# Projecting and convolving the second SSD group's B and C ahead of the first group's tiles, in both halves of a hybrid transformer block

## The chip, the cores and the metric

The kernel runs on one core of one Trainium2 chip. The metric is the device time of one execution in microseconds (us), as the median of several runs. Five engines work side by side, each on its own queue of instructions: TensorE (PE in the profile; PEld is its weight load), VectorE (DVE), ScalarE (ACT), GpSimd (POOL) and SyncE (SP), which issues most of the DMAs. One instruction of an engine waits for the results that it reads from others; whatever stands behind it in the same queue waits with it.

## The reference

One layer of a streaming encoder on 1024 tokens of width 1024, in fp32. After an RMSNorm one projection feeds three groups of heads; their outputs are concatenated, projected, normed and added, and a gated feed-forward follows:

```python
h = rmsnorm(x, pre_mix_norm)
proj = h @ w_in                       # split into the inputs of the three mixers
att = swa_sink_alibi(a_q, a_k, a_v, attn_sinks)      # sliding-window attention, 4 heads
ssd = ssd_mixer(s_z, s_xbc, s_dt, ...)               # Mamba-2 SSD, 2 groups of 4 heads
gdn = gdn_mixer(g_qkv, g_z, g_b, g_a, ...)           # gated DeltaNet, 4 heads
mix = jnp.concatenate([att, ssd, gdn], axis=-1) @ w_out
x = x + rmsnorm(mix, post_mix_norm)
h = rmsnorm(x, pre_ffn_norm)
f = (silu(h @ w_gate) * (h @ w_up)) @ w_down
x = x + rmsnorm(f, post_ffn_norm)
```

In the SSD mixer, x, B and C go through a causal convolution of four taps and a SiLU. Then, for each group, `y_diag = (C B^T * decay) x` inside a chunk, a state of 128 x 64 for each head is carried from chunk to chunk and read by C, a skip `x * D` is added, the sum is gated by `silu(z)` and normed over the 256 channels of the group. The gated DeltaNet needs the inverse of a lower triangular 128 x 128 matrix for each head and chunk of tokens.

## The kernel before, in words

The tokens are done in two halves of 512, four tiles of 128 tokens each. Within a half all three mixers are computed; the output projection of half 0 is worked in between the attention tiles of half 1; the feed-forward runs at the end for both halves.

Every fp32 product is made of three matmuls: operands are split into a high part (`wh`, `hhi`) and a low part (`wl`, `hlo`), and high x high, high x low and low x high are summed (`gemm_rows`, L207 to L209, and `gemm`, L213 to L215: three matmuls for each block of 128 rows, eight blocks a product, so 24 matmuls). A weight piece is loaded by SP (`wr_...`, L182), its high part is made by ACT (L183) and its low part in turn by POOL and DVE (L184), all under a high priority. So mm_B, mm_C and mm_x are 24 matmuls of 512 columns for one block of 128 channels of B, C or x, mm_z is 24 matmuls of 256 columns for each of four tiles of tokens, and mm_aq, mm_ak and mm_av are the attention's projections.

The order of emission in a half is a string of steps, `ORD` (L32 and L33), one for each half. Its letters: K the gated DeltaNet's keys and queries, V its values, G0 to G3 its scan over tiles; S0 and S1 the blocks of SSD group 0 and 1 (B, C, two blocks of x, then the gate z); s00 to s03 the tiles of group 0, s10 to s13 those of group 1; A the attention's projections, a0 to a3 its tiles, N the norm of the next half, O half 0's output projection. A scheduler then places each engine's instructions by a simulated timeline in which the place of emission is the priority: work that is emitted earlier goes first when it is ready, and later work fills gaps. So what stands in the string is a preference, and the order on each engine has to be looked up.

What the prediction speaks of, by lines:

- `conv_block` (L337 to L354): the product, a copy `cb` with three carried columns (ACT L344, POOL L343 or L346), the last tap with the bias (ACT L348), three taps on DVE (L350), a tanh on ACT (L353) and the gate on DVE (L354).
- `gate_rows` (L356 on): mm_z for each tile of tokens, a tanh on ACT (L363) and the gate on DVE (L364). The product's two PSUM buffers (`ps_mm`) are free again only after these.
- `decay_mats` (L439 on): the matmuls D_s (L444, L448) for two tiles of tokens and four heads, and exponentials on ACT (L453), which write E_s.
- `ssd_tile` (L659 to L725): transposes of x and B and the product C B^T into one PSUM buffer, tp_x (L688 to L690); ACT copies (L692, L694); DVE multiplies the four E_s blocks of a tile by dt and C B^T (L696, "the four E_s"); PE's y (L703, four small matmuls from E_s and xs, and L707 with the state); POOL's xw and xd (L698, L699); sz (L712), the new state (L714, or L716 and L717); y on DVE (L708, L718, L719), its square on ACT (L721), L722, a root on POOL (L167), L724 on DVE, and SP's store of the tile (L725). tp_x, D_s, y and sz take turns in two PSUM buffers (`ps_sd`).
- `gdn_diag` (L500 to L546): the inverse of the triangular matrices' diagonal blocks of 32, for all tiles of a half at once, almost all of it on DVE: a chain of products and sums in 15 steps for blocks of 16 (L525, L527), then a trip through DRAM (SP L529 to L532), then two products of four parts each (L538 with its sum L540), and back through DRAM (L545, and L558 in `gdn_inv`). `gdn_inv` (L548 on) transposes the result on DVE (L565) and makes the whole inverse of two tiles with small matmuls in a chain with ACT and DVE between them: lx (L577), lv, lX, lV.
- `gdn_scan` (L603 on): tp_v, PQ, Z, S (L642) with DVE steps between them; S is the state's product.
- `att_tile`: as (L746), the exps on ACT (L762), tp_p (L771), ao (L782).

The names in the profile carry h, t and g where the order prints them: y010 is the y of half 0, tile 1, group 0; B01 is B of half 0, group 1; Tst and Tpr are the inverse and its products.

Of the kernel before, what the change touches and what calls it, by code (L numbers as in the profile page):

```python
# [28 lines left out]
KQS = 2  # L29
SB = 2  # L30
WC = 544
ORD = ("K V G0 G1 G2 G3 S0 s00 s01 s02 s03 S1 s10 s11 s12 s13 A N a0 a1 a2 a3",  # L32
       "K V G0 G1 G2 G3 S0 s00 s01 s02 s03 S1 s10 s11 s12 s13 A a0 a1 O a2 a3")  # L33
STEPS = (1, 1, 2)
EARLY = (2, 4)
LEAD, SLEAD = 260, 90
# [33 lines left out]
def trunk(ctx, tc, a):  # L70
# [252 lines left out]
    def proj(h, hT, name, parts):  # L323
        wp = piece(f"{name}{h}", parts, KB)
        ps = ps_mm.tile([P, HT], F32, tag="mm", name=f"mm_{name}{h}")
        gemm(ps, wp, hT)
        return ps

    def proj_rows(h, hT, name, parts, width, evac):

        wp = piece(f"{name}{h}", parts, KB, width)
        for t in range(NT):
            ps = ps_mm.tile([P, HT], F32, tag="mm", name=f"mm_{name}{h}{t}")
            gemm_rows(ps[:, 0:width], hT, wp, slice(t * P, (t + 1) * P))
            evac(t, ps)

    def conv_block(h, hT, name, col, b, out):  # L337
        ps = proj(h, hT, name, [(0, w_in[:, col:col + P])])
        cb = cpool.tile([P, HT + 3], F32, tag="cb", name=f"cb_{name}{h}")
        if h == 0:  # L340
            pool.memset(cb[:, 0:3], 0.0)
        else:
            pool.tensor_copy(cb[:, 0:3], carry[:, b, :])  # L343
        act(out=cb[:, 3:], in_=ps, func=AF.Copy)  # L344
        if h == 0:
            pool.tensor_copy(carry[:, b, :], cb[:, HT:HT + 3])  # L346
        u = out
        act(out=u, in_=ps, func=AF.Identity, scale=wconv[:, b, 3:4], bias=wconv[:, b, 4:5])  # L348
        for i in (2, 1, 0):
            stt(out=u, in0=cb[:, i:i + HT], scalar=wconv[:, b, i:i + 1], in1=u,  # L350
                op0=ALU.mult, op1=ALU.add)
        th = cb[:, 0:HT]
        act(out=th, in_=u, func=AF.Tanh)  # L353
        stt(out=out, in0=th, scalar=1.0, in1=u, op0=ALU.add, op1=ALU.mult)  # L354

    def gate_rows(h, hT, name, parts, width, more=None):  # L356

        out = [ablk(f"{name}{h}{i}") for i in range(2)]
        tiles = [out[t // 2][:, t % 2 * 256:(t % 2 + 1) * 256] for t in range(NT)]

        def evac(t, ps):
            th = cpool.tile([P, HT + 3], F32, tag="cb", name=f"gth_{name}{h}{t}")[:, 0:256]
            act(out=th, in_=ps[:, 0:256], func=AF.Tanh, scale=0.5)  # L363
            stt(out=tiles[t], in0=th, scalar=1.0, in1=ps[:, 0:256], op0=ALU.add, op1=ALU.mult)  # L364
            if more is not None:
                more(t, ps)

        proj_rows(h, hT, name, parts, width, evac)
        return tiles

    def ablk(name):
        return apool.tile([P, HT], F32, tag="act", name=name)
# [418 lines left out]
    def half(h, hT, order):  # L791

        st = {}
# [23 lines left out]
            gdn_scan(st["grp"][t], st["v"])  # L817

        def ssd_blocks(g):
            blk = st[g] = {}  # L820
            for nm, b in (("B", 4 + g), ("C", 6 + g), ("x0", 2 * g), ("x1", 2 * g + 1)):
                blk[nm] = ablk(f"{nm}{h}{g}")
                conv_block(h, hT, f"{nm}{g}", O_X + b * P, b, blk[nm])
            blk["z"] = gate_rows(h, hT, f"z{g}",
                                 [(0, w_in[:, O_Z + g * 256:O_Z + (g + 1) * 256])], 256)

# [32 lines left out]
        def after():  # L859
            st["next"] = load_norm(h + 1)  # L860

        steps = dict(O=lambda: o0.append(block_first()), K=keys, V=values, G=scan, S=ssd_blocks, s=ssd, A=att_blocks, a=att, N=after)
        for step in order.split():
            steps[step[0]](*[int(c) for c in step[1:]])
        return st.get("next")

    pm_rows, o0 = [None, None], []
# [97 lines left out]
    for h in range(2):  # L965
        for t in range(GT):
            dma(vds[h][t].rearrange("h (b r) j -> (h b r) j", b=4).rearrange("(x r) j -> x r j", r=32)[:, 16:32, 0:16],
                S_bd[0:16].rearrange("p b l -> p (b l)")[:, 0:256].rearrange("p (r j) -> p r j", r=16))
    hT = half(0, hT, ORD[0])
    half(1, hT, ORD[1])  # L970
    mT_h0 = o0[0]
    for i in range(EARLY[0]):
# [91 lines left out]
    def silu(t):  # L1064
        act(out=t, in_=t, func=AF.Silu)
        return t
# [47 lines left out]
    for g in range(2):  # L1114
# [68 lines left out]
    for i in range(NP):  # L1183
        g = [silu(t) for t in ffn_pair("fg", wg, i, 0)]
# [182 lines left out]
```

## Time and profile before

| what | value |
|---|---|
| median of 3 runs | 1269.42 us (1267.31 to 1270.78) |
| the profiled execution | 1268.95 us |
| its span in the trace | 1267.2 us (1.75 us lie outside it) |
| mean granted TensorE clock | 0.982 |
| busy, TensorE / VectorE / ScalarE / GpSimd | 1218.1 / 913.7 / 574.8 / 217.8 us |

A row of a timeline has the start in us from the span's begin, the duration in us, the engine, the line, the instruction, output and inputs by the program's names, their shapes, and in brackets the idle time of the engine just before it and what ended that. "PE y L703 <- DVE E_s L696: 7.3, 2, 4.4" in the waits' view is: TensorE, at line 703, waited for VectorE's E_s of line 696, 7.3 us in all, twice, the longest 4.4. A row of windows has the stretch, its length, the busy time of PE, PEld, DVE, ACT and POOL with the number of instructions in brackets, the granted clock, the DMA engines' busy share and GB/s. In a group's row stand the shortest, median and longest duration in ns and the first and last start. Matmuls are pipelined: their spacing, not their duration, is what one costs. Group 0's tiles run from about 118 to 182 us in half 0 and from about 348 to 415 us in half 1.

### The profile page before, as it was taken

How to read it: one execution, taken by the hardware profiler on the slowest of the kernel's cores; microseconds unless marked ns; L12 is line 12 of the kernel's file. 1: busy time of each engine (PE TensorE's matmuls, PEld its weight loads, DVE VectorE, ACT ScalarE, POOL GpSimd, SP SyncE). 2: the span in 40 equal slices, each digit the busy share in tenths (PEclk: the TensorE clock that was granted, in tenths of full speed). 3: DMA queues.
4: the chain of work that ended last, by engine and by line, in shares of the span. 5: the costliest groups of instructions: out<-in, count | busy, mean ns of one | idle time of the engine just before them, and what ended most of it. 6: DMA issues, size and time to landing. Idle time of an engine off the chain costs nothing.

```text
span 1267.2 us, 18619 instructions
## 1 busy us (share of the span) xinstructions
PE 1218.1 (96%) x6384; PEld 1005.0 (79%) x6384; DVE 913.7 (72%) x1850; ACT 574.8 (45%) x1245; POOL 217.8 (17%) x313
## 2 busy tenths in 40 slices
PE   5999999999998999889999999999999999999997
PEld 4878778987787889878877888888888887888885
DVE  5677865796797385654668999886677666768885
ACT  7464435456443453553546443333433334444661
POOL 3244454233355432100000000000000000000000
PEclk9999989999998999979999999999999999999998
DMA  7333432143333222464573554542333367676315
GB/s 224 94 78 63 102 78 70 49 117 92 73 90 68 85 86 73 126 224 127 161 232 103 191 190 164 182 155 72 117 108 108 108 244 271 188 238 205 94 57 199
DMA packets 181795, 168.15 MB, mean 133 GB/s; under 512 B 52510, under 2 KB 137018, under 8 KB 181700
## 3 DMA queue, kind: packets, MB, share of 16 engines
q1 hardware_dynamic: 164276, 133.14, 36.0%
q10 hardware_dynamic: 17424, 33.82, 7.3%
q8 instruction: 50, 0.82, 0.3%
q14 instruction: 45, 0.37, 0.1%
HBM read 126.82 MB, written 40.11 MB: 132 GB/s over the span
## 4 chain that ended last, share of the span: by engine, by line
PE 82%; DVE 8%; DMA 6%; ACT 2%; issue 1%; SPq 1%; POOL 0%; ACTq 0%; DVEq 0%; POOLq 0%
PE mm_p L1238 5%; PE mm_p L1239 5%; PE mm_p L1240 5%; DMA wr_e<-in_ffn_w_gate_dram 1%; DMA x<-in_x_dram 1%; PE mm_o L208 1%; PE gram L490 1%; PE mm_o L209 1%; DMA yb<-in_ffn_w_down_dram 1%; PE mm_o L207 1%; PE y L703 1%; PE as L746 1%; PE ao L782 1%; PE mm_z L207 1%; DVE Tpr L538 1%
## 5 line engine op out<-in xcount | busy, mean ns | idle before, releaser
L167 POOL TENSOR_TENSOR rsq<-ssv,mhalf 128x1 f32<-128x1 f32 x32 | 20.0, 628 | 750.9 <-DVE ssv L260 740.3
L208 PE MATMUL mm_z<-wl_z,hhi_a 128*128 128x256 f32 x128 | 37.3, 291 | 1.6 <-DVE wl_z L184 1.6
L207 PE MATMUL mm_z<-wh_z,hhi_a 128*128 128x256 f32 x128 | 38.8, 303 | 0.0
L209 PE MATMUL mm_z<-wh_z,hlo_a 128*128 128x256 f32 x128 | 37.3, 291 | 0.0
L208 PE MATMUL mm_o<-wl_wo,hhi_m 128*128 128x256 f32 x128 | 36.7, 287 | 0.0
L209 PE MATMUL mm_o<-wh_wo,hlo_m 128*128 128x256 f32 x128 | 36.3, 284 | 0.0
L207 PE MATMUL mm_o<-wh_wo,hhi_m 128*128 128x256 f32 x128 | 36.3, 284 | 0.0
L183 ACT ACTIVATE wh_wo<-wr_wo 128x512 fp32r<-128x512 f32 x30 | 18.7, 631 | 27.2 <-PE mm_o L1133 8.2
L184 DVE TENSOR_TENSOR wl_wo<-wr_wo,wh_wo 128x512 fp32r<-128x512 f32 x22 | 15.2, 692 | 18.0 <-ACT wh_wo L183 17.9
L208 PEld LDWEIGHTS mm_z<-wl_z,hhi_a 128*128 128x128 f32 x128 | 25.6, 200 | 2.1 <-DVE wl_z L184 1.9
L207 PEld LDWEIGHTS mm_z<-wh_z,hhi_a 128*128 128x128 f32 x128 | 25.7, 201 | 0.7
L703 PE MATMUL y<-xs,E_s 128*128 128x64 f32 x128 | 19.1, 290 | 7.3 <-DVE E_s L696 7.3
L215 PE MATMUL mm_x<-hhi_a,wl_x 128*128 128x512 f32 x64 | 26.0, 406 | 0.0
L214 PE MATMUL mm_x<-hlo_a,wh_x 128*128 128x512 f32 x64 | 25.5, 398 | 0.0
L209 PEld LDWEIGHTS mm_z<-wh_z,hlo_a 128*128 128x128 f32 x128 | 25.4, 199 | 0.0
L213 PE MATMUL mm_x<-hhi_a,wh_x 128*128 128x512 f32 x64 | 25.3, 395 | 0.0
L703 PEld LDWEIGHTS y<-xs,E_s 128*128 128x128 f32 x128 | 18.1, 208 | 8.7 <-DVE E_s L696 7.7
L208 PEld LDWEIGHTS mm_o<-wl_wo,hhi_m 128*128 128x128 f32 x128 | 24.1, 189 | 1.0 <-issue 1.0
L209 PEld LDWEIGHTS mm_o<-wh_wo,hlo_m 128*128 128x128 f32 x128 | 24.1, 189 | 0.3 <-issue 0.3
L207 PEld LDWEIGHTS mm_o<-wh_wo,hhi_m 128*128 128x128 f32 x128 | 24.1, 188 | 0.3 <-ACT apT L772 0.3
L1131 PE MATMUL mm_o<-wh_wo,mhi 128*128 128x512 f32 x56 | 22.0, 393 | 0.3 <-ACT mhi L236 0.3
L207 PE MATMUL mm_gz<-wh_gz,hhi_a 128*128 128x272 f32 x64 | 20.8, 325 | 1.3 <-ACT dtn L378 1.3
(1801 smaller groups left out, 4380.8 us busy)
## 6 DMA issues: line engine op xcount, KB each, us to landing
wr_wo<-in_w_out_dram SPq DMA_DIRECT2D x32, 256.0 KB
x<-in_x_dram SPq DMA_DIRECT2D x8, 512.0 KB
wr_x<-in_w_in_dram SPq DMA_DIRECT2D x16, 256.0 KB
wr_z<-in_w_in_dram SPq DMA_DIRECT2D x16, 256.0 KB
res<-in_x_dram SPq DMA_DIRECT2D x8, 512.0 KB
resf<-x1d SPq DMA_DIRECT2D x8, 512.0 KB
mixn<-mixd SPq DMA_DIRECT2D x12, 256.0 KB
wr_e<-in_ffn_w_gate_dram SPq DMA_DIRECT2D x12, 256.0 KB
```

The lines of the kernel that those rows point to most:

```text
L167: pool.tensor_tensor(r[:, 0:n], v, mhalf[:, 0:n], op=ALU.pow)
L207: pe.matmul(ps, hi[:, tsl], whi, start=k == 0, stop=False)
L208: pe.matmul(ps, hi[:, tsl], wlo, start=False, stop=False)
L209: pe.matmul(ps, lo[:, tsl], whi, start=False, stop=k == len(wp) - 1)
L213: pe.matmul(ps, whi, hi, start=k == 0, stop=False)
L214: pe.matmul(ps, whi, lo, start=False, stop=False)
L215: pe.matmul(ps, wlo, hi, start=False, stop=k == len(wp) - 1)
L703: pe.matmul(yd[:, j], E[j], xs[:, j], start=True, stop=True)
L1131: pe.matmul(ps[t], hi[:, s], whi, start=k == korder[0], stop=False)
L1238: pe.matmul(ps[j], ah[:, s], bh, start=i == 0, stop=False)
L1239: pe.matmul(ps[j], ah[:, s], bl, start=False, stop=False)
L1240: pe.matmul(ps[j], al[:, s], bh, start=False, stop=i == NP - 1)
```

## The change

A new step, `B1`, stands behind S0 and ahead of group 0's tiles in the strings of both halves. It projects and convolves B and C of group 1 (a new function, `ssd_in`, that takes the kinds of blocks to do). When S1 comes, B and C are there, and only x and z of group 1 are done. Every block and every product stays as it is.

```diff
-ORD = ("K V G0 G1 G2 G3 S0 s00 s01 s02 s03 S1 s10 s11 s12 s13 A N a0 a1 a2 a3",
-       "K V G0 G1 G2 G3 S0 s00 s01 s02 s03 S1 s10 s11 s12 s13 A a0 a1 O a2 a3")
+ORD = ("K V G0 G1 G2 G3 S0 B1 s00 s01 s02 s03 S1 s10 s11 s12 s13 A N a0 a1 a2 a3",
+       "K V G0 G1 G2 G3 S0 B1 s00 s01 s02 s03 S1 s10 s11 s12 s13 A a0 a1 O a2 a3")
...
         def ssd_blocks(g):
-            blk = st[g] = {}
+            blk = st.setdefault(g, {})
+            if "B" not in blk:
+                ssd_in(blk, g, "BC")
+            ssd_in(blk, g, "x")
+
+        def ssd_in(blk, g, kinds):
             for nm, b in (("B", 4 + g), ("C", 6 + g), ("x0", 2 * g), ("x1", 2 * g + 1)):
+                if nm[0] not in kinds:
+                    continue
                 blk[nm] = ablk(f"{nm}{h}{g}")
                 conv_block(h, hT, f"{nm}{g}", O_X + b * P, b, blk[nm])
+            if "x" not in kinds:
+                return
             blk["z"] = gate_rows(h, hT, f"z{g}",
...
-        steps = dict(O=lambda: o0.append(block_first()), K=keys, V=values, G=scan, S=ssd_blocks, s=ssd, A=att_blocks, a=att, N=after)
+        steps = dict(B=lambda g: ssd_in(st.setdefault(g, {}), g, "BC"), O=lambda: o0.append(block_first()), K=keys, V=values, G=scan, S=ssd_blocks, s=ssd, A=att_blocks, a=att, N=after)
```

The order of the instructions shows what the scheduler makes of it. First VectorE in half 0, where the first part of the inverse ends (L525 and L527 on Tst and Tpr), before. y000 and sss000 are tile 0 of group 0, E_s000 with tp_x010 is tile 1's four E_s, wl_x0104 a low part of x's weights, B01 a tap of group 1's B:

```order
L718 TENSOR_TENSOR y000_1871<-y000_1866,xd000_1856 128x256
L527 TENSOR_REDUCE Tst0_1001<-Tpr0_1003 128x14
L714 COPY ssd_st_142<-sz000_1872 128x256
L719 TENSOR_TENSOR y000_1871<-y000_1871,z000_1694 128x256
L525 TENSOR_TENSOR Tpr0_1003<-Tst0_1001,Wst0_995 128x225
L184 TENSOR_TENSOR wl_x0104_2122<-wr_x0104_2123,wh_x0104_2121 128x512
L527 TENSOR_REDUCE Tst0_1001<-Tpr0_1003 128x15
L722 TENSOR_SCALAR sss000_1877<-sss000_1877 128x1
L525 TENSOR_TENSOR Tpr0_1003<-Tst0_1001,Wst0_995 128x256
L527 TENSOR_REDUCE Tst0_1001<-Tpr0_1003 128x16
L724 TENSOR_SCALAR y000_1871<-y000_1871,rsq_1880 128x256
L350 SCALAR_TENSOR_TENSOR B01_2018<-cb_B10_2056,wconv_98,B01_2018 128x512
```

The same place with the change:

```order
L527 TENSOR_REDUCE Tst0_1001<-Tpr0_1003 128x14
L525 TENSOR_TENSOR Tpr0_1003<-Tst0_1001,Wst0_995 128x225
L184 TENSOR_TENSOR wl_x0104_2122<-wr_x0104_2123,wh_x0104_2121 128x512
L527 TENSOR_REDUCE Tst0_1001<-Tpr0_1003 128x15
L525 TENSOR_TENSOR Tpr0_1003<-Tst0_1001,Wst0_995 128x256
L527 TENSOR_REDUCE Tst0_1001<-Tpr0_1003 128x16
L350 SCALAR_TENSOR_TENSOR B01_1832<-cb_B10_1870,wconv_98,B01_1832 128x512 x2
L184 TENSOR_TENSOR wl_x1104_2170<-wr_x1104_2171,wh_x1104_2169 128x512
L350 SCALAR_TENSOR_TENSOR B01_1832<-cb_B10_1870,wconv_98,B01_1832 128x512
L538 TENSOR_TENSOR Tpr0_1003<-Tst0_1001,Wst0_995 128x512
L354 SCALAR_TENSOR_TENSOR B01_1832<-cb_B10_1870,B01_1832 128x512
L718 TENSOR_TENSOR y000_1967<-y000_1962,xd000_1952 128x256
```

Tile 0's y chain moved from among the last steps of the first part to behind the first product of the second (L538); tile 1's four E_s (L696), which stood in the row behind the first piece, now come 13 rows behind the second. On SP tile 0's store (L725), which stood between L529 and L531, now stands behind L532. In half 1 the chain comes behind the first L538 as well.

The second place is TensorE in half 1, where the decay matrices of tiles 2 and 3 (D_s102) are made, before; mm_x111 is the second block of x and mm_z110 the first tile of z of group 1:

```order
L213 MATMUL mm_x111_4870<-hhi_a17_2723,wh_x1114_4864 128x512
L444 MATMUL D_s1020_4626<-mask_r_95,ident_r_94 128x512
L448 MATMUL D_s1020_4626<-csT1_3296,sel_r_96 128x256 x2
L214 MATMUL mm_x111_4870<-hlo_a17_2724,wh_x1114_4864 128x512
L444 MATMUL D_s1021_4634<-mask_r_95,ident_r_94 128x512
L448 MATMUL D_s1021_4634<-csT1_3296,sel_r_96 128x256 x2
L215 MATMUL mm_x111_4870<-hhi_a17_2723,wl_x1114_4865 128x512
L207 MATMUL mm_z110_4930<-wh_z110_4906,hhi_a10_2709 128x256
```

With the change:

```order
L208 MATMUL mm_z111_4958<-wl_z116_4925,hhi_a17_2723 128x256
L209 MATMUL mm_z111_4958<-wh_z116_4924,hlo_a17_2724 128x256
L444 MATMUL D_s1020_4720<-mask_r_95,ident_r_94 128x512
L448 MATMUL D_s1020_4720<-csT1_3296,sel_r_96 128x256 x2
L444 MATMUL D_s1021_4728<-mask_r_95,ident_r_94 128x512
L448 MATMUL D_s1021_4728<-csT1_3296,sel_r_96 128x256 x2
L688 MATMUL tp_x120_4736<-cst_90,x010_4298 128x128
L688 MATMUL tp_x120_4736<-cst_90,x110_4345 128x128
L689 MATMUL tp_x120_4736<-cst_90,B10_4204 128x128
L690 MATMUL tp_x120_4736<-C10_4251,B10_4204 128x128
L207 MATMUL mm_z112_4986<-wh_z110_4906,hhi_a10_2709 128x256
```

D_s moved from the end of x's second block to behind z's first two tiles (48 matmuls). In half 0 it moves from x's second block to the end of z's second tile, and tile 2's y, which stood behind 48 z matmuls, now stands behind all 96 and 14 of mm_aq.

The third place is TensorE in half 1 at the first link of the inverse's matmuls (lx10), before; mm_aq01 is the attention's first query block, y130 tile 3 of group 0:

```order
L213 MATMUL mm_aq01_5242<-hhi_a15_2719,wh_aq014_5235 128x512
L214 MATMUL mm_aq01_5242<-hlo_a15_2720,wh_aq014_5235 128x512
L577 MATMUL lx10_3862<-T210_3854,Wn10_3526 32x32 x4
L577 MATMUL lx10_3862<-T210_3854,Wn11_3565 32x32 x4
L703 MATMUL y130_4698<-xs130_4686,E_s102_4625 128x64 x4
```

With the change:

```order
L209 MATMUL mm_z113_5014<-wh_z116_4924,hlo_a17_2724 128x256
L577 MATMUL lx10_3862<-T210_3854,Wn10_3526 32x32 x4
L577 MATMUL lx10_3862<-T210_3854,Wn11_3565 32x32 x4
L688 MATMUL tp_x130_4775<-cst_90,x010_4298 128x128
L213 MATMUL mm_aq01_5242<-hhi_a10_2709,wh_aq010_5228 128x512
```

lx moved ahead of the whole query block, of which 17 matmuls stood ahead of it before. The second inverse of half 1 (tiles 2 and 3) moves from among the output projection's matmuls (mm_o) to ahead of them, and of the attention's tiles one more is done before the output projection ends.

## The prediction

> **What bounds the kernel now.** I read the page first, then TensorE's waits, the windows around the longest of them, and VectorE's (DVE's) timeline there. From the page: the span, the busy line and the chain that ended last, by engine.
>
> ```profile
> span 1267.2 us, 18619 instructions
> PE 1218.1 (96%) x6384; PEld 1005.0 (79%) x6384; DVE 913.7 (72%) x1850; ACT 574.8 (45%) x1245; POOL 217.8 (17%) x313
> PE 82%; DVE 8%; DMA 6%; ACT 2%; issue 1%; SPq 1%; POOL 0%; ACTq 0%; DVEq 0%; POOLq 0%
> ```
>
> PE is busy 1218.1 of 1267.2 us, so all its idle time is 49.1 us; the change adds and removes no arithmetic, and it can only move that idle time and the time spent at a lower clock. Three of TensorE's waits, from the view that names whom it waits for (total, times, longest):
>
> ```profile
> PE y L703 <- DVE E_s L696: 7.3, 2, 4.4
> PE tp_p L771 <- ACT asc L762: 4.5, 2, 4.0
> PE mm_z L208 <- DVE wl_z L184: 1.6, 1, 1.6
> ```
>
> The second lies in the tail of half 1's mixer. The first is in the change's reach: tile 2 of group 0 waits once in each half for its E_s. PE's timeline at those waits (start, duration, engine, instruction, idle before it):
>
> ```profile
> 147.62 0.50 PE L444 MATMUL D_s<-mask_r,ident_r 128*128 128x512 f32 x1 [0.68 <-DVE ssd_st L717]
> 157.70 0.38 PE L208 MATMUL mm_z<-wl_z,hhi_a 128*128 128x256 f32 x1 [1.65 <-DVE wl_z L184]
> 164.24 1.91 PE L703 MATMUL y<-xs,E_s 128*128 128x64 f32 x8 [2.87 <-DVE E_s L696]
> 393.59 1.97 PE L703 MATMUL y<-xs,E_s 128*128 128x64 f32 x8 [4.43 <-DVE E_s L696]
> ```
>
> The waits of 2.87 and 4.43 each cost more than themselves. The windows behind them, and a dense one (busy by engine, then granted clock):
>
> ```profile
> 161.00:171.40 10.40, 7.54 (x34) 6.97 (x33) 9.96 (x20) 1.40 (x3) 5.05 (x5) 0.67 0.12 27
> 390.00:402.00 12.00, 8.41 (x43) 8.06 (x44) 9.35 (x19) 1.78 (x4) 2.29 (x3) 0.72 0.19 30
> 440.00:480.00 40.00, 39.29 (x373) 35.18 (x371) 31.18 (x99) 19.18 (x58) 13.90 (x22) 1.00 0.25 87
> 141.25:164.96 23.71, 18.34 (x102) 14.83 (x100) 23.64 (x36) 9.16 (x23) 10.15 (x11) 0.99 0.29 69
> 367.13:394.31 27.18, 22.75 (x129) 19.16 (x127) 27.08 (x45) 11.59 (x27) 12.10 (x10) 0.98 0.33 80
> ```
>
> The clock was 0.67 over 10.40 us and 0.72 over 12.00: 0.33 x 10.40 = 3.4 and 0.28 x 12.00 = 3.4 us lost on top. So each E_s wait costs its length and about 3.4. Waits of 1.65 us and less kept the clock. The last two rows say why PE waits: DVE is busy 23.64 of 23.71 and 27.08 of 27.18 us. From the first L538 product (the second part of the triangular inverse) to tile 2's E_s, **DVE is the limiter**, and PE waits for what stands late in DVE's order. Half 0, DVE, with ScalarE's wh_x:
>
> ```profile
> 128.46 0.42 DVE L718 TENSOR_TENSOR y<-y,xd 128x256 f32<-128x256 f32 x1
> 129.39 1.34 DVE L719 TENSOR_TENSOR y<-y,z 128x256 f32<-128x256 f32 x1
> 131.17 0.69 DVE L184 TENSOR_TENSOR wl_x<-wr_x,wh_x 128x512 fp32r<-128x512 f32 x1
> 132.83 0.42 DVE L527 TENSOR_REDUCE Tst<-Tpr 128x16 f32<-128x256 f32 x1
> 133.28 1.37 DVE L724 TENSOR_SCALAR y<-y,rsq 128x256 f32<-128x256 f32 x1
> 135.24 1.11 DVE L696 SCALAR_TENSOR_TENSOR E_s<-E_s,sp,tp_x 128x128 f32<-128x128 f32 x4
> 136.93 0.68 DVE L184 TENSOR_TENSOR wl_x<-wr_x,wh_x 128x512 fp32r<-128x512 f32 x1
> 137.53 0.74 DVE L350 SCALAR_TENSOR_TENSOR B<-cb_B,wconv,B 128x512 f32<-128x512 f32 x1
> 141.25 1.08 DVE L538 TENSOR_TENSOR Tpr<-Tst,Wst 128x512 f32<-128x512 f32 x1 [2.98 <-issue]
> ```
>
> ```profile
> 130.50 0.63 ACT L183 ACTIVATE wh_x<-wr_x 128x512 fp32r<-128x512 f32 x1 [1.43 <-DMA wr_x<-in_w_in_dram]
> ```
>
> The last L527 ends at 133.25, its result goes through DRAM, and the first L538 starts at 141.25: 8.0 us. DVE fills all but 2.98 of them with tile 0's y (L719, L724), tile 1's E_s and taps of B. In half 1:
>
> ```profile
> 360.18 0.40 DVE L527 TENSOR_REDUCE Tst<-Tpr 128x16 f32<-128x256 f32 x1
> 367.13 1.05 DVE L538 TENSOR_TENSOR Tpr<-Tst,Wst 128x512 f32<-128x512 f32 x1 [1.15 <-DMA Tst<-vd]
> 368.10 0.74 DVE L350 SCALAR_TENSOR_TENSOR B<-cb_B,wconv,B 128x512 f32<-128x512 f32 x1
> 368.76 0.67 DVE L540 TENSOR_REDUCE Wst<-Tpr 128x32 f32<-128x512 f32 x1
> 369.36 1.11 DVE L696 SCALAR_TENSOR_TENSOR E_s<-E_s,sp,tp_x 128x128 f32<-128x128 f32 x4
> 396.16 0.68 DVE L540 TENSOR_REDUCE Tst<-Tpr 128x32 f32<-128x512 f32 x1
> ```
>
> Here the round trip is 6.55 us (360.58 to 367.13); the last L540, with which the inverse is ready, ends at 396.84.
>
> **Part by part.** Group 1's B and C were already projected beside tile 0; what moves is the tile work, behind them. On PE tile 0's last steps go about 8 matmuls later, tile 1's y behind 48 x products, tile 2's behind 96 z products and 14 of aq in half 0. On DVE tile 0's y chain (L718 to L724) and tile 1's E_s leave the round trip and come behind the first L538. ScalarE's copies and tanh and POOL's carries go with their blocks; the waits above show neither as a releaser here. On SP tile 0's store (L725) moves from inside the round trip to behind it, and the weights' loads keep their order.
>
> Prices, start to next start, from the rows above: product L538 0.97; reduction L540 0.60 (368.76 to 369.36); tap L350 0.66 (368.10 to 368.76); lo part 0.60 (136.93 to 137.53); from durations less the 0.08 by which these neighbours overlap, a 256-wide step 0.34 and the four E_s 1.03; L722 0.1 and L724 0.3 when no POOL work slows it (my estimates). By these, before's 36 instructions from 141.25 come to 20.9 us and took 23.7, so x1.14 in half 0; 45 instructions come to 25.5 and took 27.2, x1.06 in half 1.
>
> *Half 0, DVE.* L718, L714 and L719 no longer stand ahead of wl_x, but wl_x needs wh_x, done at 131.13: DVE idles some 1.8 us that it filled before. The last L527 then ends at 133.1, as before. Three taps and a lo part follow to 135.8, and L538 waits for the round trip: 8.0 us by half 0's row, 6.55 by half 1's; without the store in it I take 7.6, so 140.7. DVE idles 1.8 + 4.9 = 6.7 us instead of 2.98. The 16 instructions up to tile 1's E_s come to 9.9 x 1.14 = 11.3: **E_s of tile 1, E_s(1), ends at 152**. Sixteen more (10.05 x 1.14 = 11.5) lead to L718 of tile 1: 163.5. Fifteen more (8.9 x 1.14 = 10.2) to E_s(2): 173.7.
>
> *Half 0, PE.* Spacing of the products, from half 1's timeline; and two groups of half 0 with their first and last start:
>
> ```profile
> 403.76 0.28 PE L209 MATMUL mm_z<-wh_z,hlo_a 128*128 128x256 f32 x1
> 404.47 0.28 PE L209 MATMUL mm_z<-wh_z,hlo_a 128*128 128x256 f32 x1
> 404.59 0.40 PE L213 MATMUL mm_aq<-hhi_a,wh_aq 128*128 128x512 f32 x1
> 408.30 0.39 PE L214 MATMUL mm_aq<-hlo_a,wh_aq 128*128 128x512 f32 x1
> 408.63 0.69 PE L577 MATMUL lx<-T,Wn 32*32 32x32 f32 x16
> ```
>
> ```profile
> L213 PE MATMUL mm_B<-hhi_a,wh_B x8: 392/398/587, 124.2 to 130.3; 128*128 128x512 f32 x8
> L213 PE MATMUL mm_aq<-hhi_a,wh_aq x7: 392/393/394, 175.5 to 179.7; 128*128 128x512 f32 x7
> ```
>
> Six z steps take 0.71 (0.118 each), sixteen of 512 columns 3.71 (0.232). mm_B starts at 124.2; the 96 products of B, C and x at 0.232 and 1.7 us of small steps bring PE to tile 1's y at 148.2, plus 1.1 for tp_x, whose buffer waits for tile 0's L718: 149.3. So y(1) waits about 2.7 us (no wait there before), and the clock goes to half, as behind the 2.87 row: 3.4. Then y(1) 1.5 and 45 z (5.3): D_s at 162.2, waiting for L718 till 163.5: 1.3. D_s, 51 z, tp_x and 14 aq (11.6) lead to tile 2's y at 175.1, E_s(2) being ready. It ends at 176.4. Before, the same set (B, C, x, 96 z, 14 aq, tiles 0 to 2) stood at 178.2: aq from 175.5, 14 x 0.232 = 3.2, less 0.5 for tile 3's tp_x ahead of it. If DVE is quicker, half speed falls on D_s's wait and adds 3.4: 179.8. So -1.8 to +1.6; with a round trip 0.6 shorter -2.4. **I take -0.5.**
>
> *Half 1.* The second wl_x is waited for as in half 0, the last L527 ends at 362.5 to 363, and L538 starts at about 369.7 instead of 367.13: +2.6. The same count by 1.06 gives E_s(1) at 384.8 (PE there at 382.9), L718 at 394.4 (PE at 390), E_s(2) at 400.8, and the last L540 at 399.8 instead of 396.8. lx waits for it through DRAM: 6 us and 0.8 of transposing, so 406.6, and PE, without the 17 aq products that stood ahead of lx, is there at 403.8. Before, at 408.63, those 17 (3.95) and tp_x (0.5) were done: 406.6 + 4.45 - 408.63 = +2.4. Half speed behind one of these waits adds 0 to 3.4. **+3.0, from +0.5 to +5.**
>
> *Half 1, attention.* The second inverse (lx, lv, lX, lV) now runs ahead of the output projection, in a stretch of small steps (its windows row: PE busy 39.29 of 40 us, DVE 31.18); before, each link had 16 to 18 projection products behind it. One such hand-off costs:
>
> ```profile
> 454.73 0.68 PE L642 MATMUL S<-rv,kn 128*128 128x128 f32 x4 [0.71 <-DVE gpe L638]
> ```
>
> Five links at 0 to 0.7: 0 to +4; **I take two, +1.5**. The projection then ends with one attention tile fewer behind it. There the tail waits:
>
> ```profile
> 537.36 0.48 PE L771 MATMUL tp_p<-cst,asc 128*128 128x128 f32 x1 [4.04 <-ACT asc L762]
> ```
>
> That wait stays, its exps still standing behind a weight's copy on ACT; one tile's hand-offs go: -2 to +1, **-0.5**.
>
> Sum: -0.5 + 3.0 + 1.5 - 0.5 = +3.5. The profiled run took 1268.95 us (1.75 outside its span) and the median is 1269.42; on the median that is **1272.9**. The bounds' sums are -3.9 and +11.6; they will not all fall one way, so this case alone spans 1267 to 1279.
>
> The clock is what I know least. The trace has half speed behind waits of 2.87 and 4.43, none behind 1.65. [...]
>
> **The rivals.** (0.3%, 3.8 us, is about what can be told from no change.)
> *Faster, 0.26.* 96 z and 14 aq products now stand ahead of tile 2's y, so both long waits and their half speed go: 2.87 + 4.43 + 1.65 + 0.7 + 6.8 = 16.4 us. For it: E_s(2) at 173.7 is before PE in half 0. Against: the same lag then stops y(1) and D_s. It decides by their waits: if each of the four stays under about 1.9 us and keeps the clock, 7.6 comes back: 1260.6; if one half-speed stretch stays, 1264.0. I take 1263.
> *Much slower, 0.12.* DVE's lag halves the clock behind y(1) and D_s in both halves and the dense stretch stalls at each link: +3.5 + 2 x 1.7 + 2.5 = 1279 or more. It decides at waits over 1.9 us twice per half.
> *The clock's rule, 0.08:* 1269.9, as above.
> *No real move, 0.07.* The products of B and C stood beside tile 0 already; if the shifts cancel, 1269.4.
>
> **How the numbers follow.** My case has 0.47, about 0.30 of it beyond 1273.2 and 0.17 within. Slower: 0.30 + 0.12 = 0.42. Faster: 0.26. Same: 0.17 + 0.08 + 0.07 = 0.32. The range runs from the faster case's 1263 to 1279; about 2 in 10 lie outside.
>
> **What would show it.** Right: y of tile 1 and D_s (L703, L444) among the waits in both halves, near 2.8 and 1.3, and 2 and 4 us; none at tile 2's y in half 0; the first L538 at about 141 and 370 with 4 to 5 us idle before it; lx waiting near 406. Wrong: L538 earlier than 139.5 or 368, or all waits of the two stretches under 1.9 with the clock at 1.00 (the faster case); or group 0's stretch unchanged while the attention stretch moves by over 4 us.

## The result, and the profile after

The changed kernel takes 1276.01 us (median of 5 runs, 1273.22 to 1280.38), the kernel before in the same comparison 1267.31 (5 runs, 1266.94 to 1270.78): a ratio of 1.0082, with a 95% interval of 1.0055 to 1.0109. That is 7 to 14 us slower. The forecast was 1272.9, with 3.5 us lost against its 1269.42, in a range of 1263 to 1279; the sign was right, the size too small. One execution among all the runs below, of the kernel with added matmuls, took 2991.79 us, counts as slow and is left out of every time. The profiled execution took 1277.5 us, 1275.7 of them in the span. From its page: the span, the busy line, and the chain that ended last by engine.

```profile
span 1275.7 us, 18618 instructions
PE 1226.2 (96%) x6384; PEld 1012.0 (79%) x6384; DVE 914.2 (72%) x1850; ACT 577.0 (45%) x1245; POOL 217.7 (17%) x313
PE 80%; DVE 9%; DMA 6%; issue 2%; ACT 2%; SPq 1%; POOL 0%; ACTq 0%; POOLq 0%; DVEq 0%
```

The span grew by 8.5 us, and PE's busy time by 8.1, from 1218.1 to 1226.2, with the same 6384 matmuls. Its idle time stayed: 1267.2 - 1218.1 = 49.1 before, 1275.7 - 1226.2 = 49.5 now. So the loss is no waiting; the same matmuls ran slower. The mean granted clock says the same: 0.982 of full speed before, 0.973 after (0.973 to 0.977 in the five runs). Time lost to the clock is the span by what lacks of 1: 0.018 x 1267.2 = 22.8 us before, 0.027 x 1275.7 = 34.4 after, so 11.6 more. That is 3.1 more than the span grew by, so half clock doesn't always lengthen the kernel by what it takes: the first 118 us lost 1.7 us more to it than before (6.8 us at half clock against 3.4) and took no longer.

Where it was lost is seen from windows over the same five stretches of either kernel: group 0 of half 0, group 0 of half 1, the dense stretch of half 1 (the second inverse, group 1, attention), the tail of half 1's mixer, and the feed-forward part that follows it. The columns are the window and its length, busy time of PE, PEld, DVE, ACT and POOL, then the granted clock, the DMA share and GB/s. Before:

```profile
120.00:205.00 85.00, 79.63 (x511) 67.33 (x511) 62.37 (x123) 35.14 (x83) 39.38 (x51) 0.96 0.36 84
340.00:425.00 85.00, 80.57 (x518) 68.98 (x517) 62.80 (x131) 38.23 (x92) 38.07 (x44) 0.96 0.35 82
425.00:510.00 85.00, 84.29 (x720) 76.58 (x719) 55.27 (x165) 34.27 (x97) 29.97 (x44) 1.00 0.25 82
510.00:600.00 90.00, 82.23 (x448) 69.63 (x447) 48.01 (x115) 44.78 (x109) 5.83 (x9) 0.91 0.52 163
640.00:685.00 45.00, 41.14 (x184) 32.59 (x183) 32.10 (x58) 23.28 (x44) 1.63 (x3) 0.96 0.55 182
```

And after:

```profile
120.00:205.00 85.00, 80.67 (x504) 67.86 (x504) 58.98 (x114) 35.35 (x82) 36.75 (x45) 0.94 0.35 82
340.00:425.00 85.00, 80.08 (x530) 68.53 (x529) 61.98 (x129) 36.96 (x89) 34.45 (x43) 0.94 0.36 80
425.00:510.00 85.00, 84.09 (x633) 75.44 (x632) 55.01 (x166) 33.89 (x95) 28.41 (x43) 0.92 0.21 72
510.00:600.00 90.00, 80.18 (x477) 69.29 (x476) 47.55 (x113) 45.40 (x110) 8.46 (x11) 0.89 0.52 161
640.00:685.00 45.00, 41.94 (x195) 33.46 (x194) 32.75 (x62) 26.95 (x54) 3.12 (x6) 1.00 0.67 216
```

Length by lacking clock gives, stretch by stretch, 3.4, 3.4, 0, 8.1 and 1.8 us before and 5.1, 5.1, 6.8, 9.9 and 0 after. The dense stretch is the largest item: it ran at full speed before and loses 6.8 us now, and PE is as busy in it as before (84.29 and 84.09 of 85) while it gets through 633 matmuls where it got through 720 (of another mix, so the count alone is no measure of the loss).

TensorE's waits after the change, longest groups in the change's reach (total, times, longest), and PE's timeline at those of group 0 (start, duration, instruction, idle before it):

```profile
PE y L703 <- DVE E_s L696: 5.7, 3, 2.6
PE tp_p L771 <- ACT asc L762: 3.9, 1, 3.9
PE tp_x L688 <- DVE y L718: 1.9, 1, 1.9
```

```profile
143.96 0.44 PE L688 MATMUL tp_x<-cst,x 128*128 128x128 f32 x2 [1.85 <-DVE y L718]
152.67 1.97 PE L703 MATMUL y<-xs,E_s 128*128 128x64 f32 x8 [2.12 <-DVE E_s L696]
162.96 0.39 PE L444 MATMUL D_s<-mask_r,ident_r 128*128 128x512 f32 x1
175.12 1.00 PE L703 MATMUL y<-xs,E_s 128*128 128x64 f32 x8
384.21 1.63 PE L703 MATMUL y<-xs,E_s 128*128 128x64 f32 x8 [2.64 <-DVE E_s L696]
392.57 0.49 PE L444 MATMUL D_s<-mask_r,ident_r 128*128 128x512 f32 x1 [0.89 <-DVE ssd_st L717]
394.25 0.47 PE L444 MATMUL D_s<-mask_r,ident_r 128*128 128x512 f32 x1 [0.76 <-DVE y L718]
406.71 0.69 PE L577 MATMUL lx<-T,Wn 32*32 32x32 f32 x16
```

The wait for E_s moved from tile 2 to tile 1 in both halves, as forecast; tile 2's y at 175.12 waits for nothing. The eight L703 of tile 1 take 1.97 us at 152.67, those of tile 2 take 1.00 at 175.12: the first stand at half clock (0.50 from 152.6 to 159.4, 1.00 from 174 to 178). VectorE's rows show the gap that opened ahead of the first L538 product, and the wait for wh_x that was expected ahead of wl_x:

```profile
131.16 0.69 DVE L184 TENSOR_TENSOR wl_x<-wr_x,wh_x 128x512 fp32r<-128x512 f32 x1 [1.52 <-ACT wh_x L183]
141.95 1.02 DVE L538 TENSOR_TENSOR Tpr<-Tst,Wst 128x512 f32<-128x512 f32 x1 [5.14 <-issue]
369.52 1.06 DVE L538 TENSOR_TENSOR Tpr<-Tst,Wst 128x512 f32<-128x512 f32 x1 [3.87 <-DMA Tst<-vd]
```

Now the dense stretch. From PE's timeline after the change, matmuls of half 1's second inverse and what stands between and behind them, and then two groups of such matmuls from later on (the dots stand for rows left out):

```profile
458.68 0.65 PE L231 MATMUL tp_m<-cst,mixn 128*128 128x128 f32 x4
460.25 0.43 PE L703 MATMUL y<-xs,E_s 128*128 128x64 f32 x2 [0.91 <-DVE E_s L696]
460.61 0.69 PE L588 MATMUL lv<-Vd,X 32*32 32x32 f32 x16
461.23 1.14 PE L593 MATMUL lX<-T,Wn 64*64 64x64 f32 x16
462.30 0.43 PE L703 MATMUL y<-xs,E_s 128*128 128x64 f32 x2
462.57 0.28 PE L771 MATMUL tp_p<-cst,asc 128*128 128x128 f32 x1
462.78 1.71 PE L746 MATMUL as<-ak,aq 64*128 64x256 f32 x4
...
468.78 1.06 PE L588 MATMUL lv<-Vd,X 32*32 32x32 f32 x16
469.76 1.97 PE L598 MATMUL lV<-V,T 64*64 64x64 f32 x16
```

Sixteen lv matmuls take 0.69 us at 460.61 and 1.06 at 468.78, and there is a single wait, of 0.91 us. Two windows of after split the stretch at 463.2:

```profile
459.80:463.20 3.40, 2.95 (x39) 2.63 (x40) 3.27 (x12) 2.28 (x7) 0.50 (x1) 1.00 0.11 39
463.20:476.80 13.60, 13.60 (x76) 11.88 (x74) 8.07 (x23) 4.52 (x10) 4.47 (x8) 0.50 0.06 21
```

The clock is 1.00 up to 463.2 and 0.50 for the next 13.6 us, in which PE idles for nothing: 6.8 us lost, and all the half clock that this stretch has. In before the second inverse has output-projection matmuls (mm_o) among its links and its stretch is at 1.00.

The orders differ, so the same place in the two kernels is found by work done: PE's matmuls are summed, each at the spacing that its shape has in before at full clock (the median), and the times at which either kernel has reached the same sum are compared. By this count, called equal work from here on, what before does from 425 to 510 takes after 5.8 us longer.

### The profile page after: what moved, and what is told of

Same layout as the page of the kernel before. It is cut to its first block, busy times and chain, and to the rows that moved or that the text cites. A ratio compares the mean times of both kernels' runs of the same rounds, so it can differ in the third digit from the quotient of the medians.

```text
span 1275.7 us, 18618 instructions
## 1 busy us (share of the span) xinstructions
PE 1226.2 (96%) x6384; PEld 1012.0 (79%) x6384; DVE 914.2 (72%) x1850; ACT 577.0 (45%) x1245; POOL 217.7 (17%) x313
## 4 chain that ended last, share of the span: by engine, by line
PE 80%; DVE 9%; DMA 6%; issue 2%; ACT 2%; SPq 1%; POOL 0%; ACTq 0%; POOLq 0%; DVEq 0%
PE mm_p L1247 5%; PE mm_p L1248 5%; PE mm_p L1249 5%; DMA wr_e<-in_ffn_w_gate_dram 1%; PE mm_o L208 1%; PE mm_o L207 1%; PE gram L490 1%; DMA yb<-in_ffn_w_down_dram 1%; PE mm_o L209 1%; PE as L746 1%; PE ao L782 1%; PE y L703 1%; DVE Tpr L538 1%; DVE x L350 1%; PE mm_o L1140 1%
## 5 line engine op out<-in xcount | busy, mean ns | idle before, releaser
L184 DVE TENSOR_TENSOR wl_wo<-wr_wo,wh_wo 128x512 fp32r<-128x512 f32 x22 | 15.8, 719 | 19.1 <-ACT wh_wo L183 19.0
L703 PE MATMUL y<-xs,E_s 128*128 128x64 f32 x128 | 19.6, 294 | 5.7 <-DVE E_s L696 5.7
L703 PEld LDWEIGHTS y<-xs,E_s 128*128 128x128 f32 x128 | 18.4, 210 | 8.1 <-DVE E_s L696 6.5
L350 DVE SCALAR_TENSOR_TENSOR x<-cb_x,wconv,x 128x512 f32<-128x512 f32 x24 | 19.3, 804 | 5.5 <-ACT x L348 5.4
```

The costliest lines, as they stand in the source:

```text
L703: pe.matmul(yd[:, j], E[j], xs[:, j], start=True, stop=True)
```

## The experiments

The theory that they test: the loss sits in half 1, in the moved waits of group 0 and, larger, in the half clock of the dense stretch. The rivals stand in the expectations. Each ratio is against the kernel before on the same chip, and at the end of the section one table has all clocks.

**One half at a time.** The new step B1 in one half's order only. In half 0 alone:

```diff
 ORD = ("K V G0 G1 G2 G3 S0 B1 s00 s01 s02 s03 S1 ...",
        "K V G0 G1 G2 G3 S0 s00 s01 s02 s03 S1 ...")
```

> B and C ahead in half 0 alone; half 1 has the order of before. Theory A (most of the loss is a stretch of half clock in half 1, where the second inverse's small matmuls lost the projection's matmuls between them): within 0 to +2 us of before, with no half clock between 455 and 480 us; at most one half-clock window of 3.4 us (a loss of 1.7) more than before, near 197 us. Theory B (the loss is VectorE's lag in group 0's tiles, alike in both halves): about half of the loss, +4 us. By the prediction's own terms half 0 costs -0.5.

Measured: 1277.39 us (6 runs, 1275.90 to 1279.32), ratio 1.0081 [1.0065, 1.0096]. The loss was the whole one, where the theory wanted nearly none. The reason is in half 1, whose written order was not touched: the kernel's scheduler gave it another order of instructions all the same. From e1's windows around the second inverse:

```profile
455.60:459.00 3.40, 1.69 (x12) 1.20 (x12) 3.40 (x11) 1.93 (x4) 1.76 (x3) 0.99 0.02 5
459.00:476.00 17.00, 17.00 (x74) 15.76 (x73) 11.51 (x37) 4.49 (x12) 3.48 (x7) 0.50 0.18 58
```

A run of transposes and small tile steps with three short waits, of 0.79, 0.41 and 0.52 us, now stands ahead of the projection's first matmul; PE is busy half of 3.4 us there, and the next 17.0 run at half clock, 8.5 lost. So this kernel is no pure test of half 0. In half 1 alone:

```diff
 ORD = ("K V G0 G1 G2 G3 S0 s00 s01 s02 s03 S1 ...",
        "K V G0 G1 G2 G3 S0 B1 s00 s01 s02 s03 S1 ...")
```

> B and C ahead in half 1 alone. Theory A: nearly the whole loss, +6 to +9 us over before, with half clock for some 13.6 us (a loss of 6.8) between 455 and 480 us as in the changed kernel. Theory B: half of the loss, +4 us. By the prediction's own terms +4 (3.0 + 1.5 - 0.5).

Measured: 1276.31 us (6 runs, 1272.93 to 1281.23), ratio 1.0072 [1.0051, 1.0093]. As expected, half 1's step alone has nearly all the loss; half 0's adds 0.0010, 1.3 us, which the intervals don't tell from nothing. Its profiled execution is the fastest of the six (1272.93 us) and has a clock of 0.96 from 425 to 510 (3.4 lost), half of what was expected there.

**Later by one tile.** B1 behind tile 0's step instead of ahead of it, in both halves:

```diff
-       "K V G0 G1 G2 G3 S0 B1 s00 s01 s02 s03 S1 ..."
+       "K V G0 G1 G2 G3 S0 s00 B1 s01 s02 s03 S1 ..."
```

> The step stands behind tile 0 instead of ahead of it, in both halves. The projection's matmuls then stand between the links of half 1's second inverse again (8 to 24 behind each link), and tile 0's y chain comes earlier on VectorE. Theory A: no half clock between 455 and 480 us, so within 3 us of before. Theory B: VectorE's wait for the inverse's round trip is filled by tile 0's y again, and what is left of the lag decides: 0 to +4 over before.

Measured: 1278.56 us (6 runs, 1274.07 to 1281.67), ratio 1.0086 [1.0067, 1.0104]. The expectation failed. The half clock came in two places, in half 0 among transposes (tp_a, of half 1's input) with small steps between them, and in the dense stretch of half 1. Its windows there:

```profile
224.00:235.50 11.50, 11.50 (x51) 9.95 (x50) 7.85 (x23) 4.17 (x12) 5.39 (x8) 0.55 0.15 46
470.00:481.00 11.00, 11.00 (x76) 10.12 (x75) 6.65 (x27) 3.73 (x13) 3.84 (x6) 0.53 0.42 140
```

Each costs some 5 us (0.45 x 11.5, 0.47 x 11), and PE is busy throughout both. Moving the step later doesn't mend the loss; it makes another such stretch.

**Matmuls added where the clock falls.** After, with eight matmuls of 128 x 128 x 256 whose result is overwritten, four behind each of the lv steps of half 1's second inverse. They add work and change no result:

```diff
+        busy = gs[0]["h"] == 1 and i == 2
+        for _ in range(4 if busy else 0):
+            pe.matmul(p1[:, 256:512], Vd[:, 0:4].rearrange("p h c -> p (h c)"),
+                      Vd.rearrange("p h c -> p (h c)"), start=True, stop=True)
```

> The changed kernel with eight matmuls of 128x128x256 added between the links of half 1's second inverse; their result is read by nobody and the output is the same. Theory A (the half clock comes from too little work in the array): the half clock between 463 and 477 us goes or shrinks to one window, which gives back 5 to 6.8 us less what the added matmuls take (8 at about 0.45 us, 3.6 at most): 1 to 4 us faster than the changed kernel. Rival (half clock comes from VectorE's wait of 0.9 us at 460 us, or from none of this): the half clock stays, and the kernel is 3 to 4 us slower than the changed one.

Measured: 1277.84 us (5 runs, 1276.74 to 1279.14), ratio 1.0083 [1.0069, 1.0098]. The same kernel once more, for its trace:

> The same kernel as the one with eight added matmuls, for a trace, which the first run of it didn't give. Its granted clock was 0.981 in five executions against 0.975 of the changed kernel, at the same time. Theory A: the half clock of 463 to 477 us is gone, and the time it cost was taken by the added matmuls and by waits for VectorE or ScalarE that the half clock had hidden. Rival: the half clock stays there, and the clock's mean rose elsewhere.

Measured: 1277.10 us (4 runs, 1275.57 to 1277.66), ratio 1.0084 [1.0065, 1.0102]. The window with the added matmuls, and these matmuls in its timeline (the trace records each of the eight as two):

```profile
455.00:480.00 25.00, 24.10 (x233) 20.25 (x230) 18.67 (x58) 12.41 (x35) 8.17 (x13) 1.00 0.27 91
```

```profile
459.56 1.95 PE L587 MATMUL lx<-Vd 128*128 128x256 f32 x8
467.87 1.90 PE L594 MATMUL lx<-V 128*128 128x256 f32 x8
```

The half clock is gone from 455 to 480 (1.00, where after had 0.50 from 463.2 to 476.8). By equal work, the added matmuls not counted as work, the stretch from 425 to 510 takes 3.8 us longer than in before, against 5.8 in after, and the added matmuls take about 3.9: beside them nothing of the loss is left. It isn't luck of one execution either: the mean clock was 0.980 to 0.984 in the nine executions of the two runs, and 0.973 to 0.977 in the five of after. So the clock from 463 to 477 does hang on what PE is given to do: 0.50 in after, 1.00 here. The reading has two limits. The scheduler also moved other steps, lX from 461.23 to 469.70 among them, so the added matmuls aren't the only difference. And the expected 1 to 4 us did not come: 5.8 less 3.8 is 2.0 us, which these intervals can hide, and in the profiled execution the feed-forward part, at 1.00 in after, was at 0.92 from 640 to 685 (3.6 us). What makes that later half clock is open.

**The attention's start moved ahead.** A (attention's projections) ahead of group 1's tiles in half 1, so that other work lies in the dense stretch: once on after, once on before.

```diff
-       "... S0 B1 s00 s01 s02 s03 S1 s10 s11 s12 s13 A a0 a1 O a2 a3"
+       "... S0 B1 s00 s01 s02 s03 S1 A s10 s11 s12 s13 a0 a1 O a2 a3"
```

> The changed kernel with the attention's projections ahead of group 1's tiles in half 1's string. Group 0's order is the changed kernel's, matmul for matmul; in the dense stretch the output projection's matmuls (16, 19, 9 of 256 columns) stand between the links of the second inverse. Theory A (the larger part of the loss is half clock in half 1's dense stretch, which comes when transposes and matmuls of few rows follow each other without full ones; the smaller part is VectorE's lag in group 0): no half clock, or one window of it, between 440 and 490 us, and 4 to 7 us faster than the changed kernel, 1269 to 1272. Theory B (VectorE's lag in group 0 makes the whole loss): as the changed kernel, 1276.

Measured on after: 1270.65 us (12 runs, 1267.54 to 1276.74), ratio 1.0040 [1.0024, 1.0056]: half of the loss is gone, as expected. The dense stretch in its windows:

```profile
440.00:490.00 50.00, 49.65 (x452) 45.04 (x452) 38.59 (x119) 25.20 (x76) 19.07 (x30) 1.00 0.23 79
```

> The kernel before with the attention's projections ahead of group 1's tiles in half 1's string: what that move does without the step in question. Theory A: group 0 as before, with its two long waits; the dense stretch has no half clock already, so within 3 us of before, and 2 to 4 us faster than the changed kernel with the same move. Theory B: the same distance to the changed kernel with the same move as before has to the changed one, 8 us.

Measured on before: 1267.39 us (11 runs, 1264.51 to 1268.79), ratio 1.0002 [0.9987, 1.0016]. So the move by itself is worth nothing that can be told, and what it gave after came from something that only after has. With it in both, the step costs 1.0040 - 1.0002 = 0.0038, 4.8 us; without it 0.0082, 10.4 us. The difference is 5.6 us, with the four intervals taken together some 1 to 10. The dense stretch fits it: by equal work its 5.8 us are gone (-0.4 in the profiled execution of after with the move).

**VectorE relieved.** After, with the low parts of group 1's x and z weights (eight pieces) computed on GpSimd instead, so that E_s(1) comes sooner:

```diff
-            split_eng().tensor_tensor(v(lo), v(raw), f32(v(hi)), op=ALU.subtract)
+            eng = split_eng()
+            if name in ("x0104", "x1104", "z102", "z106", "x0114", "x1114", "z112", "z116"):
+                eng = pool
+            eng.tensor_tensor(v(lo), v(raw), f32(v(hi)), op=ALU.subtract)
```

> The changed kernel with the eight low parts that VectorE makes for group 1's x and z (0.6 us each, four in a half) made by GpSimd. Theory for group 0's stretch (VectorE limits there): the waits of tile 1's y and of D_s (2.1 in half 0, 2.6 and 1.65 in half 1) fall to under 1 us each, and half 1's stretch up to the first lx gets 1 to 3 us shorter. Rival (GpSimd's low parts take 1.3 to 2.7 us and PE waits for them instead): PE waits at mm_x or mm_z for wl, and the stretch is as long. The order in the dense stretch changes too, so the whole time isn't read for this.

Measured: 1291.32 us (4 runs, 1276.97 to 1292.49), ratio 1.0172 [1.0130, 1.0214]; three of the four lie above 1291. From its timelines, PE at tile 1 of half 1, VectorE's E_s for it, and GpSimd just behind (the lines are three on from those of after; L719 is the state's decay):

```profile
379.70 0.44 PE L691 MATMUL tp_x<-cst,x 128*128 128x128 f32 x2 [2.21 <-DVE ssd_st L720]
387.85 1.21 PE L706 MATMUL y<-xs,E_s 128*128 128x64 f32 x8 [0.59 <-DVE E_s L699]
397.79 0.79 PE L447 MATMUL D_s<-mask_r,ident_r 128*128 128x512 f32 x1 [3.69 <-DVE ssd_st L720]
```

```profile
387.46 1.11 DVE L699 SCALAR_TENSOR_TENSOR E_s<-E_s,sp,tp_x 128x128 f32<-128x128 f32 x4
388.44 1.26 POOL L187 TENSOR_TENSOR wl_z<-wr_z,wh_z 128x512 fp32r<-128x512 f32 x1
389.66 1.75 POOL L187 TENSOR_TENSOR wl_aq<-wr_aq,wh_aq 128x512 fp32r<-128x512 f32 x1
391.37 1.45 POOL L719 TENSOR_TENSOR ssd_st<-ssd_st,etot 128x256 f32<-128x256 f32 x1
```

The expectation failed. In half 1 the wait for E_s fell from 2.64 to 0.59 us, but not because E_s came sooner: VectorE starts it at 387.46, against 383.83 in after, 3.6 us later, of which only 2.4 come from further ahead (tile 0's last tp_x starts at 353.99 against 351.57). It was PE that came later, behind a wait of 2.21 us for the state. The state's decay now queues on GpSimd behind low parts that take 1.26 and 1.75 us, the wait for the state at D_s went from 0.89 to 3.69, and the first lx starts at 410.49 instead of 406.71. So this run moved waits to another engine and doesn't isolate VectorE's lag. That VectorE sets group 0's waits rests on its timeline, where it ends them, and on the times that were forecast from it.

**The tail.** Before, with O (half 0's output projection) behind the last attention tiles, so that it fills the tail:

```diff
-       "... S1 s10 s11 s12 s13 A a0 a1 O a2 a3"
+       "... S1 s10 s11 s12 s13 A a0 a1 a2 a3 O"
```

> The kernel before, with half 0's output projection behind all attention tiles in half 1's string, so that the last attention tiles' exps come among the projection's matmuls and not behind the weights' copies in the tail. Theory: the tail's wait for the exps (4.0 us at 537) and one stretch of half clock behind it (3.4) go: 4 to 8 us faster than before. Rival: what waits there is the projection's last tile (norm, split, transposes) in any order, and the time stays within 2 us.

Measured: 1268.43 us (12 runs, 1264.73 to 1273.16), ratio 1.0022 [1.0008, 1.0037]. The theory failed: instead of 4 to 8 us faster it is 2.8 slower. PE's timeline shows what waits in the tail now: the transposes (tp_f) of the projection's result, behind its norm, which had cover as long as attention tiles came after it:

```profile
538.00 0.87 PE L231 MATMUL tp_f<-cst,o 128*128 128x128 f32 x6 [3.08 <-ACT o L920]
543.09 2.25 PE L231 MATMUL tp_f<-cst,o 128*128 128x128 f32 x8 [4.22 <-DVE ssv L259]
```

**Both moves, without and with the step.** The order of half 1 with A ahead and O last; then the same with B1 in both halves:

```diff
+       "K V G0 G1 G2 G3 S0 [B1] s00 s01 s02 s03 S1 A s10 s11 s12 s13 a0 a1 a2 a3 O"
```

> The kernel before with both moves in half 1's string (attention's projections ahead of group 1's tiles, output projection last). Theory: as the one with the output projection last alone, within 2 us, since the first move alone gave nothing (1.0002). If the two add up otherwise, the dense stretch has changed.

Measured without the step: 1269.43 us (12 runs, 1264.71 to 1273.26), ratio 1.0021 [1.0003, 1.0039].

> The change in question with both moves: the step's own cost where neither the dense stretch nor the tail holds half clock from it. Theory (what is left of the step is VectorE's lag in group 0): 2 to 5 us slower than the same kernel without the step. Rival (the step costs nothing by itself, all was half clock elsewhere): within 1.5 us of it.

Measured with it: 1272.02 us (6 runs, 1270.74 to 1275.27), ratio 1.0054 [1.0035, 1.0073]. The step's own cost is 0.0033, 4.2 us (with both intervals some 1 to 7.5), beside the 4.8 found above with O in its old place; the forecast was 2 to 5. No version ran faster than before.

The granted clock of each profiled execution over the five stretches of the first section (window, in us), the time of the dense stretch's work (before's 425 to 510) against before by equal work, in us, and the ratio of the whole. Clocks and equal work are of one execution each:

| kernel | 120-205 | 340-425 | 425-510 | 510-600 | 640-685 | equal work | ratio |
|---|---|---|---|---|---|---|---|
| before | 0.96 | 0.96 | 1.00 | 0.91 | 0.96 | 0 | 1 |
| after | 0.94 | 0.94 | 0.92 | 0.89 | 1.00 | +5.8 | 1.0082 |
| half 0 only | 0.96 | 0.96 | 0.90 | 0.91 | 1.00 | +9.2 | 1.0081 |
| half 1 only | 0.98 | 0.96 | 0.96 | 0.89 | 1.00 | +2.7 | 1.0072 |
| behind tile 0 | 0.98 | 0.96 | 0.94 | 0.92 | 1.00 | +5.6 | 1.0086 |
| matmuls added | 0.98 | 0.96 | 1.00 | 0.92 | 0.92 | +3.8 | 1.0084 |
| after, A ahead | 0.96 | 0.96 | 1.00 | 0.89 | 1.00 | -0.4 | 1.0040 |
| before, A ahead | 1.00 | 0.96 | 1.00 | 0.92 | 0.96 | +0.8 | 1.0002 |
| low parts on GpSimd | 0.94 | 0.88 | 0.86 | 0.89 | 1.00 | +9.4 | 1.0172 |
| before, O last | 0.98 | 0.96 | 1.00 | 0.91 | 1.00 | -0.1 | 1.0022 |
| before, both moves | 0.98 | 0.96 | 1.00 | 0.89 | 1.00 | +0.1 | 1.0021 |
| step, both moves | 0.98 | 0.94 | 1.00 | 0.91 | 0.96 | -0.1 | 1.0054 |

The clock of 425-510 parts them: each kernel with less than 1.00 there is at 1.0072 or above and loses 2.7 us or more in that work, and with 1.00 there all but the one that carries the added work stay at 1.0054 or below and lose 0.8 at most.

## Why the prediction was right in sign and short in size

- **VectorE's rows in group 0.** Right. The first L538 was put at 140.7 and 369.7 and stands at 141.95 and 369.52, with 5.14 and 3.87 us idle ahead of it where "4 to 5" was said. y of tile 1 was put at 152 and 384.8 and starts at 152.67 and 384.21; its waits, put at about 2.7 and 1.9, are 2.12 and 2.64. Taking VectorE as the limiter of this stretch, and counting its instructions by neighbouring durations, was enough. The 0.3 for L724 is borne out by before's rows where GpSimd has no work beside it (0.33 to 0.35 us, at 209.62, 242.17, 420.10 and 474.40); where a low part (L184) on GpSimd has started ahead of it, L724 takes 1.36 to 1.50 (five rows, from 133.28 to 386.21).
- **Half 0, -0.5.** Half right. The wait for tile 1's D_s that was put at 1.3 us isn't there (162.96, no bracket), and tile 2's y comes at 175.12 as forecast (175.1), with about 1.5 us won against before by equal work. That the time fits so well is luck: PE came to tile 1's y 1.2 us later than forecast (152.67 less the wait of 2.12 is 150.55, not 149.3; tp_x alone waited 1.85 us and not 1.1), and this stands in for the missing 1.3. A further window of half clock, 196.9 to 200.4, then takes 1.7 back. The stretch ends within 0.5 us of before.
- **Half 1, group 0, +3.0.** Near in size, by another path. lx was put at 406.6 and starts at 406.71; by the prediction's own count that is 406.71 + 4.45 - 408.63 = +2.5, and by equal work at the end of the stretch +3.6. But PE was to be there at 403.8 and wait for the inverse, and lx waits for nothing: its input was ready at 405.74 (L565 starts on VectorE at 405.31 and takes 0.43 us), and PE itself came late, so the agreement of the two times is luck. The waits for D_s were put at 4 us in all and are 0.89 and 0.76; the half clock behind them (394.9 to 401.7, 3.4 lost) stands in their place and in that of lx's wait. Of the step's own cost of 4.8 and 4.2 us by the two pairs of experiments, equal work puts 4.3 and 3.3 in this stretch.
- **Half 1, attention, +1.5 from 0 to +4.** This is the term that failed. The prediction counted five links at 0 to 0.7 us of waiting. The waiting came to 0.91 us, in its bounds; what it left out is the clock: from 463.2 to 476.8, transposes and small matmuls (lv of 32 rows, lV of 64) with no projection between them ran at 0.50, with no wait longer than that. By equal work it is +5.8, by the windows 6.8, by the pairs of experiments 5.6. The row that it built on, PE busy 39.29 of 40 us at 1.00, was of before, where the projection lay in it: busy time was carried over, the kind of matmul was not.
- **The tail, -0.5.** Wrong in sign: +1.8 by equal work, and the clock went from 0.91 to 0.89 there (1.8 us). Its wait of 4.04 stayed, as forecast: 3.90 at 549.16. No experiment took this stretch alone, so its cause stays open.
- **Unforeseen gains.** The feed-forward part lost 1.7 us to the clock in before's profile, at 655.8, and none in after's: about -2.6 by equal work. Before with O last has no half clock there either (1.00 from 640 to 685), and before with A ahead has it (0.96). So it comes and goes without the step; what decides it was not shown, and the gain can't be counted on.
- **The rivals.** The faster case needed the four waits under 1.9 us; 2.12 and 2.64 decide against it. The "much slower" one had two of three parts: half clock behind y(1) in both halves, and the dense stretch losing; but at each link it put waits, and there were none, and its sign, waits over 1.9 us twice in a half, did not come. The clock's rule, at 1269.9, lies 3.0 us below the forecast, and no run shows a term for that; in after, waits of 2.12 us (ended at 152.67), 2.64 (at 384.21) and 0.91 (at 460.25) have half clock behind them, from 152.6, 384.7 and 463.2.

Sum, by equal work (before's 0 to 118, 118 to 205, 205 to 348, 348 to 425, 425 to 510, 510 to 600 and the rest): start 0.0, half 0 +0.2, up to half 1's group 0 -0.2, group 0 of half 1 +3.6, dense +5.8, tail +1.8, feed-forward -2.6: the 8.5 us of span, beside the measured 7 to 14.

## What to carry to other kernels

A move that adds no waiting in all can still slow TensorE: before work is taken out of a stretch to fill another, ask which matmuls are left in it. In the dense stretch here those that were left ran at 0.50 for 13.6 us, and with eight matmuls of 128 x 128 x 256 among them the clock was 1.00. Read the granted clock by windows in before and after ahead of the waits; here the idle time stayed within 0.4 us, and only the clock showed the loss. Where a scheduler orders the instructions, a change in one place is compared over the whole program, since the stretch that pays may be one whose order nobody touched.

## What the runs showed of the hardware

In half 0 of after the clock fell without idle time ahead of it. Two windows side by side:

```profile
193.50:196.90 3.40, 3.40 (x39) 2.38 (x38) 1.04 (x4) 1.55 (x5) 0.55 (x1) 1.00 0.34 82
196.90:200.40 3.50, 3.50 (x9) 2.69 (x10) 0.00 (x0) 2.87 (x9) 0.58 (x1) 0.51 0.12 37
```

PE is busy for all of 193.5 to 196.9, with a wide matmul at its start, then the lv matmuls of 32 rows, lX of 64 rows and D_s, whose second part (L448) has 24, and the next 3.5 us have a clock of 0.51. From 25 us on, the trace of after has half clock from 26.3, 152.6, 196.9, 384.7, 394.9, 463.2 and 548.5, for 6.8, 6.8, 3.4, 3.4, 6.8, 13.6 and 20.5 us; that of before from 27.7, 164.3, 393.0, 536.3, 546.6 and 655.8, for 3.4, 6.8, 6.8, 6.8, 10.2 and 3.4. Neither busy time nor idle time by itself tells where: ahead of 196.9 PE is busy for all of 3.4 us and half clock follows, and in before it waits 1.65 us at 157.70 and the clock is 1.00 from 147 to 160. With the added matmuls one stretch went from 0.50 to 1.00; what brings half clock on and what ends it was not tested beyond that.

So the same wait has no fixed price. Tile 2's wait for E_s in half 0 is 2.87 us in before and in before with A ahead. Behind it 3.4 us were lost to the clock in before and none with A ahead; in the latter, from its windows and timeline:

```profile
162.00:176.00 14.00, 11.13 (x80) 10.15 (x80) 13.30 (x25) 4.65 (x12) 6.12 (x7) 1.00 0.17 30
```

```profile
165.43 1.21 PE L703 MATMUL y<-xs,E_s 128*128 128x64 f32 x8 [2.87 <-DVE E_s L696]
```

Before has a clock of 0.76 over the same 162 to 176.
